# The opening of a transformer layer: modulation and the first token half first, then two tile pairs of products in one run

## The chip, the cores and the metric

The kernel runs on one core of a Trainium2 chip. TensorE multiplies matrices into PSUM; VectorE, ScalarE and GpSimd work elementwise; SyncE and ScalarE issue the transfers from HBM that are named here. The metric is the device time of one execution in microseconds (us). Three timed runs of the kernel before took 1918.53, 1914.31 and 1918.40 us, median 1918.4. The profiled execution is a fourth, of 1915.77 us; its span from the first to the last recorded instruction is 1914.0 us.

## What the kernel computes

One encoder layer on x of 1024 tokens by 1024 channels in float32: a half-step SwiGLU feed-forward, a mixer (convolution and attention), and a second half-step feed-forward. Each is modulated by a conditioning vector c. Cut to what the change touches:

```python
c_act = jax.nn.silu(c)
mod = (c_act @ w_ada[l] + b_ada[l]).reshape(B, N_SUBLAYERS, 3, D)    # 3 x (shift, scale, gate)

def post_norm_sublayer(x, mod, weight, f, g, b):
    shift, scale, gate = mod[:, 0, None, :], mod[:, 1, None, :], mod[:, 2, None, :]
    y = f(x * (1.0 + scale) + shift)
    return layer_norm(ALPHA * x + weight * (1.0 + gate) * y, g, b)

def swiglu(h, w_in, w_out):                     # h: 1024 x 1024, w_in: 1024 x 5632
    gate, up = jnp.split(h @ w_in, 2, axis=-1)
    return (jax.nn.silu(gate) * up) @ w_out
```

Ahead of the first product stand shift and scale of the first sub-layer: 2048 columns of `w_ada`, 8 MB. With them h = x * A + B is made, A = 1 + scale and B = shift, one number per channel.

## The kernel before

**Products.** The first projection h @ w_in runs in 22 tile pairs j (128 gate columns and 128 up columns each). For each pair the 2x2 block product (two halves of the channels, two halves of the tokens) is done with seven products instead of eight, and each of the seven in four channel blocks with three float32 terms (high x high, low x high, high x low): 84 products of 128x512 per pair, called p1 to p7 in the code. Their left factors come from the weights: `ah`/`al` (high and low part of the raw weights), and `sf` (sums of weights) with its parts `sh`/`sl`. The right factors come from the tokens: for each channel block kk, `r_kbh`/`r_kbl` are the parts of the first token half's h, `r_kb` those of one quarter of the second half's h, and `r_kt1h/l` and `r_kt3h/l` those of the differences t12 and t34 between the two halves' h (T1 to T4). A high part is a cast on ScalarE, the low part the rest on VectorE (`split`). Sums of products are gathered in PSUM under names as fi_0A, fi_0S (tile 0), fi_1A (tile 1).

**The opening.** There are four column blocks kk of 256 channels. For each: `first_ada` fetches its `w_ada` columns (four transfers of 512 KB), `first_x` both token halves (`xc`, two of 512 KB); `first_mod` sums eight 128-row pieces of `w_ada` times `c_act`, some columns on VectorE (`ada0a`) and some on TensorE (128x1 products into `ada0p`), and VectorE adds the bias to get two columns of B and two of A. `first_t` transposes both token halves on TensorE, `first_h` applies A and B on ScalarE and VectorE, `right_first`, `right_second` and `right_third` make the right factors, with GpSimd doing most of the subtractions, and `go(k)` issues the 12 products of this block for four of tile 0's seven products (A11, A12, S2, S1). Then `in_phase` does the rest of tile 0, tile 1 and so on; VectorE and ScalarE apply the gate and make the next tile's weight factors beside it.

**What sets the order.** The order of issue is written out by hand in `SEQ` (line 44): `a0` fetches block 0's columns, `M03` computes them (the last digit sets how many of four columns VectorE sums), `w0` fetches tile 0's weights, `x0` the tokens, `G0` and `S0` make weight factors, `H0` is transposes and h, `R0...` the right factors (a letter per step for VectorE or GpSimd), `g0` the products. Each engine then takes its instructions in the order of its own queue, and waits by semaphores for others; a scheduler places instructions within these queues. All transfers named here are in SyncE's queue, in the order of `SEQ`; `slot` and the pools give buffers, and a transfer into a buffer waits until its last reader is through. Tile 1's weights are fetched after the last of `SEQ`, and their factors are issued after block 3's last split.

Of the kernel before, what the change touches and what calls it, by code (L numbers as in the profile page):

```python
# [14 lines left out]
P = 128  # L16
# [27 lines left out]
SEQ = "a0 M03 w0 x0 G0 a1 H0d x1 R0VGVGV M12 x2 a2 H1 M24 S0 g0 a3 R1VGVGG H2 g1 x3 R2VGVGG M33 H3d R3VVVGV g2 g3"  # L44
# [4 lines left out]
def layer_kernel(ctx, tc, a, out):  # L49
# [39 lines left out]
    S.activation(c_act, c_raw, AF.Silu)  # L89
# [216 lines left out]
    def in_load(wp, s, w_in, j):  # L306
# [6 lines left out]
        for dst, src in ((ra[:, 0], k1[:, :, g]), (ra[:, 1], k2[:, :, g]), (rb, k1[:, :, u]), (ra[:, 2], k2[:, :, u])):  # L313
            SY.dma_start(dst, src)
# [9 lines left out]
    def in_sums(wp, s, j, raws, left, eng=V, order=(0, 1)):  # L324
# [3 lines left out]
        sf = [wp.tile([P, 2, 4, P], F32, tag="sf", bufs=2, name=f"sf{s}_{j}_{i}") for i in range(2)]  # L328
        eng.tensor_tensor(sf[0][:, 0], rb, ra[:, 2], ALU.add)
        eng.tensor_tensor(sf[0][:, 1], sf[0][:, 0], ra[:, 0], ALU.subtract)  # L330
        eng.tensor_tensor(sf[1][:, 0], ra[:, 0], rb, ALU.subtract)
        eng.tensor_tensor(sf[1][:, 1], ra[:, 1], sf[0][:, 1], ALU.subtract)
# [333 lines left out]

    x_in = a["x"][0]
    with pool("p1a") as wp:
# [4 lines left out]

        def first_ada(kk):
            raws = []
            for m in range(2):
                for q in range(2):
                    name = f"ada0_{kk}_{m}{q}"
                    if kk == 0 or kk == 3 and m == 1:
                        raw = slot(name, (P, 4, 256), F32)  # L680
                    else:
                        raw = wp.tile([P, 4, 256], F32, tag="sl" if q else "sh", bufs=3, name=name)
                    SY.dma_start(raw, w_ada[:, 4 * q : 4 * q + 4, m * D + kk * 256 : m * D + (kk + 1) * 256])
                    raws.append(raw)
            return raws

        def first_x(kk):
            cols = slice(kk * 256, (kk + 1) * 256)
            xc = []
            for half in range(2):  # L690
                x = slot(f"xc{kk}_{half}", (P, 4, 256), F32)
                SY.dma_start(x, x_in[half * H : (half + 1) * H, cols].rearrange("(t p) n -> p t n", p=P))
                xc.append(x)
            return xc

        def first_mod(kk, raws, n):

            ps = wide(f"ada0p{kk}")
            if n:
                acc = wp.tile([P, 2, 256], F32, tag="ada_acc", bufs=1, name=f"ada0a{kk}")  # L700
            parts = [(m, max(0, 4 - n - 2 * m) * P) for m in (0, 1)]
            for j in range(KD):
                for m, lo in parts:
                    if lo >= 256:
                        continue
                    raw, dst = raws[2 * m + j // 4][:, j % 4, lo:], acc[:, m, lo:]
                    if j == 0:
                        V.tensor_scalar(dst, raw, c_act[:, 0:1], None, ALU.mult)
                    else:
                        V.scalar_tensor_tensor(dst, raw, c_act[:, j : j + 1], dst, ALU.mult, ALU.add)  # L710
            for m, lo in parts:
                for e in range(2):
                    es = slice(e * P, (e + 1) * P)
                    o = ps[:, 2 * m + e : 2 * m + e + 1]
                    if e * P >= lo:
                        PE.matmul(o, lhsT=acc[:, m, es], rhs=ones[:, 0:1], start=True, stop=True)
                        continue
                    for j in range(KD):
                        PE.matmul(
                            o, lhsT=raws[2 * m + j // 4][:, j % 4, es], rhs=c_act[:, j : j + 1],  # L720
                            start=j == 0, stop=j == KD - 1,
                        )
            ks = slice(2 * kk, 2 * kk + 2)
# [3 lines left out]
        def first_t(kk, xc, half):  # L727
            ps = wide(f"hT0_{kk}_{half}")
            for e in range(2):
                for i in range(4):  # L730
                    o = e * H + i * P
                    PE.transpose(ps[:, o : o + P], xc[half][:, i, e * P : (e + 1) * P], ident)
            return ps

        def first_h(kk, ps, half, HD):
            h = slot(f"h0_{kk}_{half}", dt=F32)
            k = 2 * kk
            h_of(h[:, 0], ps[:, 0:H], A0, B0, k)
            if HD:
                V.tensor_scalar(h[:, 1], ps[:, H:T], A0[:, k + 1 : k + 2], B0[:, k + 1 : k + 2], ALU.mult, ALU.add)  # L740
            else:
                h_of(h[:, 1], ps[:, H:T], A0, B0, k + 1)
            return h

        def early(wp, s, w_in, ops):
            order = (("A11", "B11"), ("A12", "B21"), ("S2", "T2"), ("S1", "T1"))
            begun = {}
            ada, xs_, hs, w, L0 = {}, {}, {}, [], {}

            def go(k):  # L750
                for left, right in order:
                    if left not in begun:
                        begun[left] = bank(f"fi{s}_0{left}")
                    product(begun[left], L0[left], ops[right], (k,))

            for tok in SEQ.split():
                c, k, v = tok[0], int(tok[1]), tok[2:]
                if c == "a":  # L760
                    ada[k] = first_ada(k)
                elif c == "x":
                    xs_[k] = first_x(k)
                elif c == "w":
                    w.append(in_load(wp, s, w_in, 0))
                elif c == "G":
                    L0.update(in_gate(wp, s, 0, w[0]))
                elif c == "S":
                    in_sums(wp, s, 0, w[0], L0, G if v else V)
                elif c == "M":  # L770
                    first_mod(k, ada[k], int(v))
                elif c == "H":
                    for half in range(2):
                        hs[k, half] = first_h(k, first_t(k, xs_[k], half), half, v == "d")
                elif c == "R":
                    e = [{"V": V, "G": G}[n] for n in v]
# [690 lines left out]
```

## Time and profile before

| | us |
|---|---|
| Timed runs, median (1914.31 to 1918.53) | 1918.4 |
| Profiled execution | 1915.77 |
| Its span | 1914.0 |
| TensorE busy | 1828.2 (96%) |
| VectorE busy | 1463.4 (76%) |
| ScalarE busy | 773.6 (40%) |
| GpSimd busy | 325.6 (17%) |
| First product of tile 4 starts at | 141.7 |

The mean granted clock of TensorE is 0.979 of full speed. In the profile's rows PE is TensorE, PEld its weight loads (they lie beside PE), DVE is VectorE, ACT ScalarE, POOL GpSimd, SP SyncE; L140 is line 140 of the kernel. A row in order of time begins with the start and the duration in us; in square brackets stands how long the engine had nothing to do before it, and what ended that. A product's duration includes the way through the array, so that products overlap; the distance of their starts (the pitch) is what one costs in a dense run. The same names (r_0bh, fi_0A) return in the second feed-forward, so a count of 4 for a name can hold instructions of both.

### The profile page before, as it was taken

The page shows a single profiled execution, that of the slowest core. Times are in us where ns is not written, and L with a number is a line of the kernel's source. Part 1 is how long each engine was busy: PE and PEld are TensorE (multiplying, and loading weights), DVE is VectorE, ACT ScalarE, POOL GpSimd, SP SyncE. Part 2 cuts the span into 40 slices and gives each one's busy share as a digit, 9 for nine tenths or more (in the row PEclk, how much of TensorE's full clock was granted, in tenths as well). Part 3 has the DMA queues.
Part 4 walks back from the last instruction along what each step waited for, and adds up shares of the span by engine and source line. Part 5 has one row for each costly group of instructions (what it writes and reads, how often), then busy time and mean ns, then how long its engine had stood idle before and what let it go on. Part 6 is the DMA issues. An engine that isn't in the chain of part 4 may idle for free. (4 is left out here: it accounts for less than half of the span.)

```text
span 1914.0 us, 23141 instructions
## 1 busy us (share of the span) xinstructions
PE 1828.2 (96%) x8562; PEld 1513.0 (79%) x8562; DVE 1463.4 (76%) x1982; ACT 773.6 (40%) x1233; POOL 325.6 (17%) x259
## 2 busy tenths in 40 slices
PE   5899999999999999999999889979999999999997
PEld 5688888888888878878788677857888888888886
DVE  8867667766698878999888768688777565569888
ACT  3423333332445442133277664353333333354540
POOL 3200000000000020057667541260000000000001
PEclk7899999999999999999999999989999999999999
DMA  8536555442885324111000014125555333188432
GB/s 254 165 99 208 163 161 175 158 149 83 296 301 165 113 61 163 46 35 33 11 2 1 12 45 154 67 67 170 168 172 177 121 110 127 39 285 281 127 121 72
DMA packets 203696, 246.76 MB, mean 129 GB/s; under 512 B 14122, under 2 KB 124831, under 8 KB 203582
## 3 DMA queue, kind: packets, MB, share of 16 engines
q1 hardware_dynamic: 200234, 235.81, 38.6%
q0 software_dynamic: 2112, 7.34, 1.0%
q10 hardware_dynamic: 1236, 2.13, 0.3%
q8 instruction: 67, 1.10, 0.2%
q14 instruction: 47, 0.39, 0.1%
HBM read 188.08 MB, written 57.15 MB: 128 GB/s over the span
## 5 line engine op out<-in xcount | busy, mean ns | idle before, releaser
L563 PE MATMUL fo<-wr,gl 128*128 128x512 f32 x1848 | 422.5, 390 | 0.5 <-DVE pv L606 0.4
L563 PEld LDWEIGHTS fo<-wr,gl 128*128 128x128 f32 x1848 | 346.2, 188 | 74.8 <-DVE pv L606 0.8
L140 DVE TENSOR_TENSOR sl<-sf,sh 128x1024 fp32r<-128x1024 f32 x87 | 109.3, 1257 | 118.5 <-ACT sh L139 118.5
L139 ACT CAST sh<-sf 128x1024 fp32r<-128x1024 f32 x88 | 92.7, 1054 | 210.0 <-issue 35.8
L910 DVE SCALAR_TENSOR_TENSOR cacc<-u,convw,cacc 128x1009 f32<-128x1009 f32 (+14 forms) x120 | 151.5, 1324 | 0.2
L373 POOL DMA_DIRECT2D gd<-gf x8 | 4.6, 573 | 824.4 <-DVE gf L439 823.9
L140 DVE TENSOR_TENSOR gl<-gr,gl 128x512 fp32r<-128x512 f32 x148 | 102.3, 698 | 7.2 <-ACT gl L139 5.8
L139 ACT CAST gl<-gr 128x512 fp32r<-128x512 f32 x148 | 90.5, 618 | 23.2 <-DMA gr<-gd 16.5
L153 DVE SCALAR_TENSOR_TENSOR ada<-adaw,c_act,ada 128x512 f32<-128x512 f32 x98 | 73.3, 748 | 32.9 <-DMA adaw<-in_w_ada_dram 31.9
L215 POOL TENSOR_TENSOR rr<-rv,mhalf 128x1 f32<-128x1 f32 x24 | 21.8, 909 | 410.3 <-DVE rv L213 408.9
L1036 DVE TENSOR_REDUCE mx<-sc 128x1 f32<-128x1024 f32 x64 | 76.3, 1216 | 19.2 <-PE sc L1034 19.2
L1038 ACT ACTIVATE p<-sc,mx 128x1024 f32<-128x1024 f32 x64 | 71.6, 1122 | 45.1 <-DVE mx L1036 44.9
L139 ACT CAST ah<-ra 128x1536 fp32r<-128x1536 f32 x44 | 65.1, 1479 | 58.0 <-DMA ra<-in_ffn_w_in_dram 14.3
L140 DVE TENSOR_TENSOR al<-ra,ah 128x1536 fp32r<-128x1536 f32 x44 | 77.1, 1752 | 1.6 <-ACT ah L139 1.4
L401 ACT ACTIVATE gf<-gf 128x512 f32<-128x512 f32 x44 | 27.8, 632 | 120.8 <-DVE gf L400 114.9
L139 ACT CAST wr<-wa 128x512 fp32r<-128x512 f32 x66 | 41.2, 624 | 74.3 <-PE fo L563 73.7
L140 DVE TENSOR_TENSOR wr<-wa,wr 128x512 fp32r<-128x512 f32 x66 | 45.5, 690 | 26.6 <-ACT wr L139 26.3
L891 PE MATMUL glu<-hm,gluh 128*128 128x512 f32 x256 | 65.6, 391 | 0.0
L1090 POOL TENSOR_TENSOR p<-p,p 128x1024 f32<-128x1024 f32 x27 | 65.0, 2408 | 1.8
L139 ACT CAST wr<-wb 128x512 fp32r<-128x512 f32 x66 | 40.2, 620 | 60.4 <-PE fo L563 49.7
L1107 PE MATMUL av<-vf,aT 128*128 128x128 f32 x512 | 63.2, 277 | 1.0 <-ACT cacc L1172 1.0
L1107 PEld LDWEIGHTS av<-vf,aT 128*128 128x128 f32 x512 | 60.6, 194 | 1.5 <-ACT cacc L1172 1.3
(3490 smaller groups left out, 4735.9 us busy)
## 6 DMA issues: line engine op xcount, KB each, us to landing
gr<-gd SPq DMA_DIRECT2D x148, 256.0 KB, 3.4
ra<-in_ffn_w_in_dram SPq DMA_DIRECT2D x132, 256.0 KB, 3.7
adaw<-in_w_ada_dram SPq DMA_DIRECT2D x56, 512.0 KB, 3.9
gd<-gf SPq DMA_DIRECT2D x102, 256.0 KB, 2.1
rb<-in_ffn_w_in_dram SPq DMA_DIRECT2D x44, 256.0 KB, 3.7
wb<-in_ffn_w_out_dram SPq DMA_DIRECT2D x44, 256.0 KB, 5.0
wa<-in_ffn_w_out_dram SPq DMA_DIRECT2D x44, 256.0 KB, 5.1
gd<-s SPq DMA_DIRECT2D x40, 256.0 KB, 2.0
```

Of the source, the lines that this page charges most:

```text
L139: a = S.copy(hi, x)
L140: b = eng.tensor_tensor(lo, x, hi.bitcast(F32), ALU.subtract)
L153: V.scalar_tensor_tensor(acc, raw[:, jj], c_act[:, n : n + 1], acc, ALU.mult, ALU.add)
L215: G.tensor_tensor(r, v, mhalf[:, 0:1], ALU.pow)
L401: S.activation(c0, c0, AF.Silu)
L563: PE.matmul(ps, lhsT=g[:, x, ts_], rhs=w[:, y], start=n in (1, 2, 3) and k == i == 0, stop=k == NK - 1 and i == 2, skip_group_check=n not ...
L891: PE.matmul(q[2 * m + h], lhsT=w[:, m * P : (m + 1) * P], rhs=hm[k][h][:, x], start=k == 0 and n == 0, stop=k == KD - 1 and n == 2,)
L910: V.scalar_tensor_tensor(acc[:, lo_t:hi_t], u[:, lo_t + sh : hi_t + sh], convw[:, i, jj : jj + 1], acc[:, lo_t:hi_t], ALU.mult, ALU.add,)
L1036: V.tensor_reduce(mx_, ps, axis=AX.X, op=ALU.max, negate=True)
L1038: S.activation(pe, ps, AF.Exp, bias=mx_, accum_out=sm[:, e : e + 1])
L1090: last = G.tensor_tensor(p0, p0, p1, ALU.add)
L1107: PE.matmul(ps[:, 0:P], lhsT=aT[:, kt], rhs=vf[kt][:, h * P : (h + 1) * P], start=kt == 0, stop=kt == 7)
```

## The change

The fetches are put in another order: first, for each block, eight transfers of 256 KB of `w_ada` and the first token half; then the second halves of blocks 0 and 1, tile 1's weights, and the second halves of blocks 2 and 3. Tile 0's weights are fetched by ScalarE's queue, after `c_act`. `first_mod` treats all four columns alike: VectorE sums 2n of the eight pieces over 512 columns (n = 3 in all blocks: six pieces), TensorE adds the other two and the sum, and ScalarE adds the bias of each column out of PSUM. Only the first token half is transposed there. Nothing of `go(k)` is left; a block's TensorE work is issued after the columns of the block before. What follows is in `mid`, which `in_phase` calls with the steps of the first two tiles: their products in one run, with the second halves' transposes between them and all subtractions on VectorE. `rows`, a pool of one row buffer, is allocated earlier, and t12 of block 0 lies in it. `in_sums` can make its two pairs of sums at different times.

```diff
-SEQ = "a0 M03 w0 x0 G0 a1 H0d x1 R0VGVGV M12 x2 a2 H1 M24 S0 g0 a3 R1VGVGG H2 g1 x3 R2VGVGG M33 H3d R3VVVGV g2 g3"
+NV = (3, 3, 3, 3)
...
+            for q in range(4):
+                raw = slot(f"ada0_{kk}_{q}", (P, 2, 2, 256), F32)
+                for m in range(2):
+                    src = w_ada[:, 2 * q : 2 * q + 2, m * D + kk * 256 : m * D + (kk + 1) * 256]
+                    SY.dma_start(raw[:, :, m], src)
...
         def first_mod(kk, raws, n):
 
-            ps = wide(f"ada0p{kk}")
...
-            V.tensor_tensor(B0[:, ks], ps[:, 0:2], bcol(0, 0)[:, ks], ALU.add)
-            V.scalar_tensor_tensor(A0[:, ks], ps[:, 2:4], 1.0, bcol(0, 1)[:, ks], ALU.add, ALU.add)
+            ps = bank(f"ada0p{kk}")
+            acc = slot(f"ada0a{kk}", (P, 2, 2, 256), F32)[:, 0]
+            for j in range(2 * n):
+                raw = raws[j // 2][:, j % 2]
+                if j == 0:
+                    V.tensor_scalar(acc, raw, c_act[:, 0:1], None, ALU.mult)
+                else:
+                    last = V.scalar_tensor_tensor(acc, raw, c_act[:, j : j + 1], acc, ALU.mult, ALU.add)
+            for i in range(4):
+                m, es = i // 2, slice(i % 2 * P, (i % 2 + 1) * P)
+                o = ps[:, i : i + 1]
+                for j in range(2 * n, KD):
+                    PE.matmul(
+                        o, lhsT=raws[j // 2][:, j % 2, m, es], rhs=c_act[:, j : j + 1], start=j == 2 * n, stop=False
+                    )
+                pe = PE.matmul(o, lhsT=acc[:, m, es], rhs=ones[:, 0:1], start=n == 4, stop=True)
+                k = 2 * kk + i % 2
+                to, bias = ((B0, bcol(0, 0)), (A0, bada1))[m]
+                S.activation(to[:, k : k + 1], o, AF.Identity, bias=bias[:, k : k + 1], scale=1.0)
+            return last.ins, pe.ins
...
+            with tc.issue_after(c_silu.ins):
+                raws = [in_load(wp, s, w_in, 0, S)]
+            ada, xb = [], []
+            for kk in range(4):
+                ada.append(first_ada(kk))
+                xb.append(first_x(kk, 0))
+            xc = [first_x(kk, 1) for kk in range(2)]
+            raws.append(in_load(wp, s, w_in, 1))
+            xc.extend(first_x(kk, 1) for kk in range(2, 4))
+            hb, L = [], [{}, {}]
+            for kk in range(4):
+                with tc.issue_after(columns) if kk else nullcontext():
+                    summed, columns = first_mod(kk, ada[kk], NV[kk])
+                    hb.append(first_h(kk, xb[kk], 0))
+                copied, rest = right_first(f"r0_{kk}", ops, hb[kk])
...
+            with tc.issue_after(first["pe"]):
+                st[0][1]()
+                hc.extend(first_h(kk, first["xc"][kk], 1) for kk in range(2))
+                with tc.issue_after(flipped[-1]):
+                    st[0][2]()
+                for kk in range(4):
...
+                    V.tensor_tensor(t[:, 0], h[:, 0], b[:, 0], ALU.subtract)
+                    V.tensor_tensor(t[:, 1], h[:, 1], t[:, 0], ALU.subtract)
+                    t12.append(t)
+                    if kk:
+                        copied, rest = right_t(f"r0_{kk - 1}", ops, 1, t12[kk - 1])
...
+            for kk in range(5):
+                if kk < 4:
+                    b, h, t = hb[kk], hc[kk], t12[kk]
+                    right_b22(f"r0_{kk}", ops, h)
+                    V.tensor_tensor(h[:, 0], h[:, 1], h[:, 0], ALU.subtract)
+                    V.tensor_tensor(h[:, 1], b[:, 1], t[:, 1], ALU.subtract)
+                if kk:
+                    copied, rest = right_t(f"r0_{kk - 1}", ops, 3, hc[kk - 1])
+            for n in (7, 3, 4):
+                st[0][n]()
...
+            for n in (7, 3, 4):
+                st[1][n]()
```

VectorE's queue before, from block 0's right factors on. `ada0a_296` and `ada0a_362` are the sums of blocks 1 and 2, `r_0t1l` and `r_0t3l` low parts of differences:

```order
L140 TENSOR_TENSOR r_0bl<-h_0_0_255,r_0bh 128x1024
L710 SCALAR_TENSOR_TENSOR ada0a_296<-ada_1_11_244,c_act,ada0a_296 128x256 x2
L140 TENSOR_TENSOR r_0t1l<-r_0t_278,r_0t1h 128x1024
L140 TENSOR_TENSOR r_0b_288<-h_0_1_267,r_0b_288 128x512
L724 TENSOR_TENSOR B_107<-ada0p_295,bada 128x2
L725 SCALAR_TENSOR_TENSOR A_106<-ada0p_295,bada 128x2
L708 TENSOR_SCALAR ada0a_362<-ada_2_00_329,c_act 128x256
L140 TENSOR_TENSOR r_0t3l<-r_0t_285,r_0t3h 128x1024
L710 SCALAR_TENSOR_TENSOR ada0a_362<-ada_2_00_329,c_act,ada0a_362 128x256 x3
```

VectorE's queue after, from the end of block 1's sums (`ada0a_325`) over block 2's (`ada0a_365`) to block 2's low part:

```order
L712 SCALAR_TENSOR_TENSOR ada0a_325<-ada_1_1_213,c_act,ada0a_325 128x512 x2
L712 SCALAR_TENSOR_TENSOR ada0a_325<-ada_1_2_216,c_act,ada0a_325 128x512 x2
L142 TENSOR_TENSOR r_1bl<-h_1_0_357,r_1bh 128x1024
L710 TENSOR_SCALAR ada0a_365<-ada_2_0_224,c_act 128x512
L712 SCALAR_TENSOR_TENSOR ada0a_365<-ada_2_0_224,c_act,ada0a_365 128x512
L712 SCALAR_TENSOR_TENSOR ada0a_365<-ada_2_1_227,c_act,ada0a_365 128x512 x2
L712 SCALAR_TENSOR_TENSOR ada0a_365<-ada_2_2_230,c_act,ada0a_365 128x512 x2
L142 TENSOR_TENSOR r_2bl<-h_2_0_397,r_2bh 128x1024
```

Before, pieces of one block's sums stood between low parts of another's factors. Now all sums of block 1 come first, then r_1bl, and behind it all sums of block 2; the adds that make A and B are gone from this queue.

TensorE's queue before, the first products of tile 0 (fi_0A, fi_0S) between transposes (hT) and the columns of blocks 1 and 2 (`ada0p`):

```order
L352 MATMUL fi_0A_399<-r_0bh,ah_0_234 128x512
L732 MATMUL hT_1_0_337<-ident,xc_0_270 128x128 x7
L716 MATMUL ada0p_295<-ones,ada0a_296 128x1 x2
L732 MATMUL hT_1_0_337<-ident,xc_0_270 128x128
L352 MATMUL fi_0A_399<-r_0bl,ah_0_234 128x512
L352 MATMUL fi_0A_399<-r_0bh,al_0_235 128x512
L352 MATMUL fi_0A_403<-r_0bh,ah_0_234 128x512
L352 MATMUL fi_0A_403<-r_0bl,ah_0_234 128x512
L352 MATMUL fi_0A_403<-r_0bh,al_0_235 128x512
L732 MATMUL hT_1_1_349<-ident,xc_1_272 128x128 x8
L352 MATMUL fi_0S_407<-r_0t1h,sh_0_0_391 128x512
L352 MATMUL fi_0S_407<-r_0t1l,sh_0_0_391 128x512
```

TensorE's queue after, from the last columns of block 3 (`ada0p_404`) on:

```order
L717 MATMUL ada0p_404<-c_act,ada_3_3_247 128x1 x2
L720 MATMUL ada0p_404<-ones,ada0a_405 128x1
L717 MATMUL ada0p_404<-c_act,ada_3_3_247 128x1 x2
L720 MATMUL ada0p_404<-ones,ada0a_405 128x1
L360 MATMUL fi_0A_444<-r_0bh,ah_0_306 128x512
...
L360 MATMUL fi_0A_444<-r_3bh,ah_0_306 128x512
L731 MATMUL hT_0_1_460<-ident,xc_1_252 128x128 x5
L360 MATMUL fi_0A_444<-r_3bl,ah_0_306 128x512
L360 MATMUL fi_0A_444<-r_3bh,al_0_307 128x512
L731 MATMUL hT_0_1_460<-ident,xc_1_252 128x128 x3
L731 MATMUL hT_1_1_472<-ident,xc_1_254 128x128 x8
L360 MATMUL fi_0A_484<-r_0bh,ah_0_306 128x512
```

All columns stand ahead of the first product, and the second halves' transposes (hT_0_1, hT_1_1) stand behind it.

TensorE's queue before, at the first products with the last difference, r_3t3 (`sh_0_1` and `sl_0_1` are weight factors of tile 0):

```order
L352 MATMUL fi_0S_407<-r_2t3h,sl_0_1_396 128x512
L352 MATMUL fi_0S_407<-r_3t3h,sh_0_1_395 128x512
L352 MATMUL fi_0S_407<-r_3t3l,sh_0_1_395 128x512
L352 MATMUL fi_0S_407<-r_3t3h,sl_0_1_396 128x512
L352 MATMUL fi_0S_411<-r_0b_288,sh_0_1_395 128x512 x2
```

TensorE's queue after, at the same products:

```order
L360 MATMUL fi_0S_600<-r_3b_675,sh_0_1_320 128x512 x2
L360 MATMUL fi_0S_600<-r_3b_675,sl_0_1_321 128x512
L360 MATMUL fi_0A_444<-r_3t3h,sh_0_1_320 128x512
L360 MATMUL fi_0A_444<-r_3t3l,sh_0_1_320 128x512
L360 MATMUL fi_0A_444<-r_3t3h,sl_0_1_321 128x512
L360 MATMUL fi_0A_444<-r_0t3h,ah_0_306 128x512
```

The first product that reads r_3t3l is the 119th of the run after the change, with both tiles' first four products of the seven and tile 0's p7 around it. Before, it stood among tile 0's alone.

## Rows read from the trace of the kernel before

**Rows 1.** Stages: length, busy us (instructions) by engine, clock, DMA share, GB/s

```profile
5.00:20.00 15.00, 9.96 (x53) 9.47 (x53) 12.43 (x27) 3.96 (x4) 1.00 (x1) 1.00 1.12 337
20.00:30.00 10.00, 7.39 (x36) 6.41 (x36) 8.97 (x13) 3.56 (x4) 4.24 (x4) 0.55 1.10 348
30.00:51.70 21.70, 14.21 (x49) 11.29 (x48) 21.52 (x34) 9.43 (x12) 8.97 (x5) 0.58 0.59 184
...
65.20:75.30 10.10, 7.96 (x16) 4.50 (x17) 8.69 (x11) 5.58 (x7) 2.25 (x2) 0.51 0.17 48
75.30:102.10 26.80, 26.80 (x118) 21.89 (x117) 25.43 (x35) 9.89 (x13) 0.00 (x0) 0.99 0.57 162
...
141.70:1914.00 1772.30, 1713.05 (x8062) 1419.55 (x8061) 1353.32 (x1821) 721.02 (x1169) 296.41 (x236) 0.99 0.39 125
```

**Rows 2.** TensorE in time: start us, us, instruction [idle before <-releaser]

```profile
30.25 0.63 PE L352 MATMUL fi_0A<-r_0bh,ah 128*128 128x512 f32 x1
30.68 0.63 PE L352 MATMUL fi_0A<-r_0bl,ah 128*128 128x512 f32 x1
...
58.92 1.04 PE L732 MATMUL hT<-ident,xc 128*128 128x128 f32 x8
59.71 0.47 PE L352 MATMUL fi_0A<-r_2bh,al 128*128 128x512 f32 x1
...
65.18 1.10 PE L352 MATMUL fi_0A<-r_3bh,ah 128*128 128x512 f32 x2 [3.40 <-ACT r_3bh L139]
...
70.16 1.22 PE L352 MATMUL fi_0S<-r_3t1h,sh 128*128 128x512 f32 x2 [0.77 <-ACT r_3t1h L139]
```

**Rows 3.** VectorE in order of time, its kinds of instruction

```profile
10.01 2.56 DVE L710 SCALAR_TENSOR_TENSOR ada0a<-ada,c_act,ada0a 128x256 f32<-128x256 f32 x5
13.68 0.16 DVE L724 TENSOR_TENSOR B<-ada0p,bada 128x2 f32<-128x2 f32 x1 [1.10 <-PE ada0p L716]
...
55.78 2.28 DVE L140 TENSOR_TENSOR r_2bl<-h,r_2bh 128x1024 fp32r<-128x1024 f32 x1
...
79.40 1.22 DVE L140 TENSOR_TENSOR sl<-sf,sh 128x1024 fp32r<-128x1024 f32 x1
80.53 0.68 DVE L417 TENSOR_TENSOR p<-fi_0S,p 128x512 f32<-128x512 f32 x1
81.13 1.22 DVE L140 TENSOR_TENSOR sl<-sf,sh 128x1024 fp32r<-128x1024 f32 x1
...
91.83 0.48 DVE L151 TENSOR_SCALAR ada<-adaw,c_act 128x512 f32<-128x512 f32 x1
...
96.21 0.75 DVE L153 SCALAR_TENSOR_TENSOR ada<-adaw,c_act,ada 128x512 f32<-128x512 f32 x1
...
98.68 1.53 DVE L153 SCALAR_TENSOR_TENSOR ada<-adaw,c_act,ada 128x512 f32<-128x512 f32 x2
```

**Rows 4.** First products of tiles 2, 3, 4: count, ns, first and last start

```profile
L352 PE MATMUL fi_2A<-r_0bh,ah x4: 389/389/389, 102.1 to 1311.3; 128*128 128x512 f32 x4
...
L352 PE MATMUL fi_3A<-r_0bh,ah x4: 388/389/389, 121.2 to 1330.5; 128*128 128x512 f32 x4
...
L352 PE MATMUL fi_4A<-r_0bh,ah x4: 389/389/476, 141.7 to 1349.5; 128*128 128x512 f32 x4
```

**Rows 5.** TensorE in order of time, first modulation columns and transposes

```profile
12.63 1.01 PE L716 MATMUL ada0p<-ones,ada0a 128*128 128x1 f32 x4 [3.33 <-DVE ada0a L710]
14.83 1.54 PE L732 MATMUL hT<-ident,xc 128*128 128x128 f32 x6 [1.19 <-DMA xc<-in_x_dram]
```

**Rows 6.** ScalarE in order of time, its kinds of instruction

```profile
2.69 0.21 ACT L89 ACTIVATE c_act<-c_raw 128x8 f32<-128x8 f32 x1
13.29 1.47 ACT L139 CAST ah<-ra 128x1536 fp32r<-128x1536 f32 x1 [10.39 <-DMA ra<-in_ffn_w_in_dram]
...
18.82 1.03 ACT L139 CAST r_0bh<-h 128x1024 fp32r<-128x1024 f32 x1
...
30.18 1.45 ACT L251 ACTIVATE h<-hT,B,A 128x512 f32<-128x512 f32 x2 [3.84 <-DVE A L725]
```

More of the change, by code (lines that the diff above doesn't have):

```diff
@@ L2 @@
+from contextlib import nullcontext
 import concourse.bass as bass
@@ L327, in in_sums @@
             eng = G
[L328 to L332, printed above, removed]
+        if order[0] == 0:
+            left["sf"] = [wp.tile([P, 2, 4, P], F32, tag="sf", bufs=2, name=f"sf{s}_{j}_{i}") for i in range(2)]
+        sf = left["sf"]
+        if 0 in order:
+            eng.tensor_tensor(sf[0][:, 0], rb, ra[:, 2], ALU.add)
+            eng.tensor_tensor(sf[0][:, 1], sf[0][:, 0], ra[:, 0], ALU.subtract)
+        if 1 in order:
+            eng.tensor_tensor(sf[1][:, 0], ra[:, 0], rb, ALU.subtract)
+            eng.tensor_tensor(sf[1][:, 1], ra[:, 1], sf[0][:, 1], ALU.subtract)
         for i in order:
@@ L664, in out_phase @@
             after(1, k)
+    rows = tc.alloc_tile_pool(name="rows", bufs=1, reuse_waits="tile", side="right")
     x_in = a["x"][0]
@@ L672, in layer_kernel @@
         B0 = const.tile([P, KD], F32, name="B0")
+        bada1 = const.tile([P, KD], F32, name="bada1")
+        V.tensor_scalar(bada1, bcol(0, 1), 1.0, None, ALU.add)
         def first_ada(kk):
             raws = []
[L676 to L684, printed above, removed]
@@ L727, in first_t, with first_x @@
-        def first_t(kk, xc, half):
+            for q in range(4):
[3 more added lines that the diff above has]
+                    SY.dma_start(raw[:, :, m], src)
+                raws.append(raw)
+            return raws
+        def first_x(kk, half):
+            x = slot(f"xc{kk}_{half}", (P, 4, 256), F32)
+            src = x_in[half * H : (half + 1) * H, kk * 256 : (kk + 1) * 256]
+            SY.dma_start(x, src.rearrange("(t p) n -> p t n", p=P))
+            return x
@@ L728, in first_t, with first_h @@
+        def first_h(kk, x, half):
             ps = wide(f"hT0_{kk}_{half}")
@@ L731, in first_t @@
                     o = e * H + i * P
-                    PE.transpose(ps[:, o : o + P], xc[half][:, i, e * P : (e + 1) * P], ident)
-            return ps
-        def first_h(kk, ps, half, HD):
+                    flipped[:] = [PE.transpose(ps[:, o : o + P], x[:, i, e * P : (e + 1) * P], ident).ins]
             h = slot(f"h0_{kk}_{half}", dt=F32)
[L737 to L742, printed above, removed]
+            for e in range(2):
+                h_of(h[:, e], ps[:, e * H : (e + 1) * H], A0, B0, 2 * kk + e)
@@ L743, in first_h @@
             return h
+        first, flipped = {}, []
         def early(wp, s, w_in, ops):
[L746 to L776, printed above, removed]
-                    right_first(f"r0_{k}", ops, hs[k, 0], e[0])
-                    t12 = right_second(f"r0_{k}", ops, hs[k, 0], hs[k, 1], e[1], e[2])
-                    last = right_third(f"r0_{k}", ops, hs[k, 0], hs[k, 1], t12, e[3], e[4])
-                elif c == "g":
-                    go(k)
```

85 lines of the change are left out of this document (41 added, 44 removed).

## The prediction

> **What bounds the kernel now.** I read the stage table first [rows 1]. From 75.3 us on TensorE is busy 26.80 of 26.80 us, and from 141.7 us 1713.05 of 1772.30, at a granted clock of 0.99: what counts there is the number of products and their pitch. The change touches only what comes before. Between 20 and 51.7 us the granted clock is about half (0.55, 0.58), and a product takes 0.43 us from its start to the next one's, 30.25 to 30.68 [rows 2]. VectorE is busy 21.52 of 21.70 us in the stretch from 30, and the DMA engines only 0.59 of it: VectorE sets the pace, not the fetch. Part of its load is its neighbour's: at 55.78, in a time when GpSimd subtracts, a 128x1024 low part takes 2.28 us, and at 79.40, with GpSimd at rest, 1.22 [rows 3]. Then TensorE stands still for 3.40 us ahead of 65.18 [rows 2], and the next 10.1 us run at a clock of 0.51 [rows 1].
>
> Tile pairs start at 102.1, 121.2 and 141.7 us for tiles 2, 3 and 4 [rows 4]. One pair is 84 products, and 121.2 - 102.1 = 19.05 us (0.227 per product). Tile 3 takes 20.5, so 1.5 us more, for convolution constants and modulation columns between its products. The instruction order is the same in both kernels from tile 3's first product on, and ahead of tile 4 both have 336 products and 64 transposes. So the question is one number: when does tile 4's first product start, 141.7 us now.
>
> **The change part by part.** After it, products start only when all four column blocks of modulation are through. I call that moment T0.
>
> Block 0. The first token half has the same 3.7 MB ahead of it, so it lands as now, at 14.8 [rows 5]. Eight transposes at half clock: 6 took 1.54, the pitch is 0.215, so 1.65 us, to 16.5. Then four modulation columns. TensorE makes one, ScalarE adds the bias from PSUM (a 128x1 instruction), and since all four share a bank, TensorE's next column waits for ScalarE's read. Two raw products and one of ones: now four columns take 1.1 us from VectorE's last add to VectorE's read, 12.57 to 13.68 [rows 3, 5], so 0.35 for the first and 0.2 for each further single product. I take 0.45 for the first, since its raw products are done, 0.85 for each later one (three products and the hand-over), and 0.25 for ScalarE's part: 0.7, then 1.1 each. The third column is read at 16.5 + 2.9 = 19.4. Then h, the fourth column's read 0.17, and h again (two take 1.45), the high part 1.05 and a hand-over 0.1 [rows 6]: 22.2. VectorE then makes three 128x1024 low parts at a pitch of 1.13 (79.40 to 80.53 [rows 3]), of which two are the weights': 25.6.
>
> Blocks 1 to 3. VectorE adds six eighths of the fetched weights: one 128x512 at 0.48 and five dependent ones at 1.53 - 0.75 = 0.78 [rows 3], 4.4 us in all, to 30.0 for block 1. What is queued behind it decides the period: the low part r_1bl stands in VectorE's queue ahead of block 2's adds, and it waits for columns (2.9), h and the fourth column (1.62), and the high part (1.15), which is 5.7 us without work for VectorE. The period is 5.7 + 1.1 + 4.4 = 11.2. Block 3's adds end at 30.0 + 2 x 11.2 = 52.4. The last column comes 3.7 later: **T0 = 56.1**. The fetch is not in the way: weights, 4 x 2.5 MB of blocks and what else precedes come to 11.5 MB, 33 us at 348 GB/s [rows 1], and block 3's adds start at 48. ScalarE now issues tile 0's four weight fetches itself; it has 10.39 us without work there [rows 6], so they cost nothing.
>
> Cost of the unknown. A 128x1 ScalarE instruction from PSUM isn't in the trace. From below it is bounded by VectorE's 128x2, 0.16, and from above by ScalarE's 128x512 from PSUM, 0.73 (half of 1.45); the nearest row is ScalarE's own 128x8, 0.21 [rows 3, 6], which I take. Some 16 of them are on the path to T0: 16 x (0.16 - 0.21) = -0.8 and 16 x 0.52 = +8.3 us are the ends. [...]
>
> From T0 to tile 4. Four pairs of 84 products: 4 x 19.05 = 76.2. Tile 3's extras 1.5. The second halves' 32 transposes, now in the dense part: 8 took 0.79 at full clock (58.92 to 59.71 [rows 2]), 3.2. The clock: I take half for the columns' stage, as between 20 and 51.7, and a dense start at 70.16 got full clock at 75.3 [rows 1, 2], 5.1 us later: 12 products at 0.43 instead of 0.23, 2.4 in all. Stalls: GpSimd's 16 instructions are now VectorE's, without the slow-down by the neighbour. VectorE can begin them when the first transposed second half is through ScalarE, some ten products and five transposes at half clock and one h after T0: 4.3 + 1.0 + 0.8 and hand-overs, T0 + 7. Up to the low part of the last difference, r_3t3l, it has 24 instructions of 128x512 at 0.60 (80.53 to 81.13; 14.4), nine of 128x1024 at 1.14 (10.3), one half as long again (1.7), and two of the gate row at 0.4 (0.8; the kind at 91.83) [rows 3]: 27.2, and 0.4 for results that the next instruction waits for, T0 + 34.6. TensorE comes to the product that needs it, its 119th, at 118 x 0.227 + 2.4 + 3.2 = T0 + 32.4. Wait 2.2. For the other first uses (tile 1's A22 and its second pair of sums, tile 2's first weights) I add 1.5, as VectorE and ScalarE run without a gap there: 3.7. Between no stall and twice that is the range of this term.
>
> Sum: 76.2 + 1.5 + 3.2 + 2.4 + 3.7 = 87.0; 56.1 + 87.0 = 143.1 against 141.7, **1.4 us later**. Where the gain goes: the 3.40 us of standing still and the half clock of 20 to 75 are gone, but the 48 products of tile 0 that lay in that time are now paid after it. Behind T0 the fetch has one new place: the gate row's fetch waits in SyncE's queue for a slot that VectorE frees at about T0 + 28, and tile 3's weights stand behind it. They have tile 2's 19 us of products as cover; without it 1 to 2 us.
>
> The profiled execution took 1915.8 us (span 1914.0); the median of the runs is 1918.4. I put the change on their middle, 1917.1: **1918.5 us**. About 0.3%, 5.75 us, is what a measurement can tell from no change.
>
> **The rivals.** (A) *The fetch sets the pace.* If the blocks overlap, VectorE works on one block's adds while the others' columns run, a block costs 1.1 + 4.4 = 5.5, adds end at 41, and T0 is 44 to 45: 12 us less, 1906.5. Against it is the queue order above (r_1bl ahead of block 2's adds); for it only that the data is there. (B) *The clock stays full.* The rows show full clock between 5 and 20 us with TensorE busy 9.96 of 15, and 0.55 from 20 on [rows 1]. If columns and transposes hold it, 12 column waits shrink by 0.3, and the 2.4 of the cold start go: 6 us less, 1912.5. (C) *Slower.* Place: the wait for r_3t3l. If VectorE is another 2 us late there (a dependent pair of subtractions per block waits on its own result), TensorE stands for 4.2 us. The one idle time with a fall behind it is the 3.40 us ahead of 65.18; if such a one comes, 10.1 us at half pitch follow [rows 1, 2], 24 products, 24 x 0.2 = 4.8. Then 2.0 + 4.8 = 6.8 more, 1925.3. [...] Against (C): my sum has only 2.2 there, and no row shows that so short a gap decides. (D) *It doesn't do what it says:* column reads near 0.5 rather than 0.21 keep TensorE and ScalarE alternating, 16 x 0.3 = 5 us later, 1923.5, and VectorE idle still longer.
>
> **How the numbers follow.** Forecast 0.55; A 0.07; B 0.14; C 0.15; D 0.09. Faster than 1912.6: A, half of B, a little of the forecast: 0.15. Slower than 1924.2: C, a third of D, a little of the forecast: 0.20. Within: 0.65. The forecast's own range is 1914.5 to 1922.5 (stalls 0 to 7.4). The whole range leaves out A and the far end of the column price: 1911 to 1928.
>
> **What would show it.** TensorE's first product at about 56 us and tile 4's at about 143. Blocks 11 us apart, with VectorE waiting some 5.7 us for ScalarE's high part before each r_1bl, r_2bl, r_3bl, and TensorE's columns waiting on ScalarE. Granted clock near 0.5 until about 61, then 1.0. A wait of some 2 us ahead of the first product with r_3t3l. I am wrong if blocks come 5 to 6 us apart (A), if the load stage shows full clock (B), if a stretch at half clock follows after 88 (C), or if tile 4 onward differs by more than 2 us from now.

## The result and the profile after

The changed kernel took 1930.22 us (median of four runs, 1929.06 to 1930.87) beside 1917.88 for the kernel before: 1.0067 times as long, 95% interval 1.005 to 1.0085. It is slower by 12 us; the forecast was 1918.5 with a range of 1911 to 1928. The profiled execution has a span of 1929.1 us, 15.1 more than before.

Nearly all of it lies ahead of tile 4. The first row is the first product of tile 0, the second that of tile 4, in the changed kernel (count; shortest, median and longest in ns; first and last start):

```profile
L360 PE MATMUL fi_0A<-r_0bh,ah x4: 398/476/774, 67.8 to 1265.6; 128*128 128x512 f32 x4
...
L360 PE MATMUL fi_4A<-r_0bh,ah x4: 389/389/476, 155.9 to 1363.3; 128*128 128x512 f32 x4
```

Tile 4 starts at 155.9 us and not at 141.7 [rows 4]: 14.2 later. T0, the first product, is at 67.8; I had put it at 56.1. From there to tile 4 are 88.1 us, and I had put 87.0. So the stretch from T0 to tile 4 came out within 1.1 us of the sum, and the opening took 11.7 us more than I thought. The stages of the changed kernel (columns as in [rows 1]):

```profile
20.00:30.00 10.00, 6.24 (x28) 5.67 (x27) 4.49 (x6) 5.28 (x8) 0.00 (x0) 1.00 1.10 348
30.00:51.70 21.70, 10.39 (x44) 9.57 (x44) 9.53 (x13) 4.17 (x9) 0.00 (x0) 1.00 1.11 314
51.70:67.80 16.10, 9.53 (x43) 8.79 (x42) 5.38 (x7) 4.68 (x9) 0.00 (x0) 1.00 0.00 1
```

Between 30 and 51.7 VectorE was busy 21.52 us [rows 1] and is now busy 9.53. The fetch moves 314 GB/s to 51.7 and then nothing: in the 16 us before T0 every byte that the opening needs is there. No engine is full and nothing is fetched, so it is a chain that sets the time. One link of it is block 1's columns on TensorE, in order of time (start us, us, instruction, and the idle time ahead with what ended it):

```profile
34.38 0.59 PE L720 MATMUL ada0p<-ones,ada0a 128*128 128x1 f32 x2 [7.44 <-DVE ada0a L712]
35.32 1.02 PE L717 MATMUL ada0p<-c_act,ada 128*128 128x1 f32 x4 [0.35 <-ACT B L723]
36.19 0.56 PE L720 MATMUL ada0p<-ones,ada0a 128*128 128x1 f32 x2
37.11 1.01 PE L717 MATMUL ada0p<-c_act,ada 128*128 128x1 f32 x4 [0.35 <-ACT B L723]
```

A round, from one column's first product to the next one's, is 37.11 - 35.32 = 1.79 us, where I had 1.1. L717 is two products and the row says x4; L720 is one and the row says x2. The group of the columns' tile says it for the whole opening:

```profile
L717 PE MATMUL ada0p<-c_act,ada x64: 344/352/374, 12.8 to 67.2; 128*128 128x1 f32 x64
...
L720 PE MATMUL ada0p<-ones,ada0a x32: 213/352/372, 18.5 to 67.6; 128*128 128x1 f32 x32
```

The program has 2 x 4 x 4 = 32 products on L717 and 16 on L720. Each float32 product of one column stands as two instructions. The row on which I priced a column, "L716 ... x4" in 1.01 us [rows 5], was therefore two columns and not four. The kernel before has the same two for one: the last digits of `M03`, `M12`, `M24` and `M33` make 3 + 2 + 4 + 3 = 12 products of ones, and its trace has 24 records of them:

```profile
L716 PE MATMUL ada0p<-ones,ada0a x24: 250/352/373, 8.5 to 55.4; 128*128 128x1 f32 x24
```

What the longer rounds do to a block is seen on ScalarE and VectorE. ScalarE in block 1, in order of time:

```profile
36.80 0.26 ACT L723 ACTIVATE B<-ada0p,bada 128x1 f32<-128x1 f32 x1 [1.53 <-PE ada0p L720]
38.59 0.26 ACT L723 ACTIVATE A<-ada0p,bada 128x1 f32<-128x1 f32 x1 [1.53 <-PE ada0p L720]
38.88 0.78 ACT L253 ACTIVATE h<-hT,B,A 128x512 f32<-128x512 f32 x1
40.38 0.26 ACT L723 ACTIVATE A<-ada0p,bada 128x1 f32<-128x1 f32 x1 [0.72 <-PE ada0p L720]
40.68 0.78 ACT L253 ACTIVATE h<-hT,B,A 128x512 f32<-128x512 f32 x1
41.49 1.04 ACT L141 CAST r_1bh<-h 128x1024 fp32r<-128x1024 f32 x1
```

And VectorE from the end of block 1's sums to block 2's low part:

```profile
30.43 3.90 DVE L712 SCALAR_TENSOR_TENSOR ada0a<-ada,c_act,ada0a 128x512 f32<-128x512 f32 x5
42.56 1.23 DVE L142 TENSOR_TENSOR r_1bl<-h,r_1bh 128x1024 fp32r<-128x1024 f32 x1 [8.24 <-ACT r_1bh L141]
43.70 0.48 DVE L710 TENSOR_SCALAR ada0a<-ada,c_act 128x512 f32<-128x512 f32 x1
44.22 3.90 DVE L712 SCALAR_TENSOR_TENSOR ada0a<-ada,c_act,ada0a 128x512 f32<-128x512 f32 x5
56.36 1.22 DVE L142 TENSOR_TENSOR r_2bl<-h,r_2bh 128x1024 fp32r<-128x1024 f32 x1 [8.24 <-ACT r_2bh L141]
```

VectorE waits 8.24 us for each high part, not 5.7: a period of 13.8 us (42.56 to 56.36), not 11.2. A read of one column is 0.26 us, close to the 0.21 that I took. The second half of h waits for the fourth column (0.72 us of idle time at 40.38), which I had hidden beside the first half.

### The profile page after: what moved, and what is told of

Same layout as the page of the kernel before. It is cut to its first block, busy times and chain, and to the rows that moved or that the text cites. A ratio compares the mean times of both kernels' runs of the same rounds, so it can differ in the third digit from the quotient of the medians.

```text
span 1929.1 us, 23148 instructions
## 1 busy us (share of the span) xinstructions
PE 1828.7 (95%) x8570; PEld 1514.3 (78%) x8570; DVE 1451.3 (75%) x1952; ACT 780.8 (40%) x1254; POOL 298.3 (15%) x243
## 5 line engine op out<-in xcount | busy, mean ns | idle before, releaser
L141 ACT CAST wr<-wa 128x512 fp32r<-128x512 f32 x66 | 41.2, 624 | 73.9 <-PE fo L571 71.8
```

Of the source, the lines that this page charges most:

```text
L141: a = S.copy(hi, x)
```

## The experiments

Each was timed beside the kernel before, whose medians in the four sessions were 1915.5, 1916.1, 1916.7 and 1916.2, and 1917.9 beside the change; so between sessions the ratios are the safer comparison. T0 is the start of the first product of the dense run; where products stand between the blocks there is none.

| Run | T0 | tile 4 | time | ratio to before, 95% interval |
|---|---|---|---|---|
| before | | 141.7 | | |
| the change | 67.8 | 155.9 | 1930.2 | 1.0067 [1.005, 1.0085] |
| e1_four_sums | 62.1 | 151.0 | 1923.3 | 1.0036 [1.0023, 1.0049] |
| e2_banks | 53.1 | 141.9 | 1914.6 | 0.9995 [0.9986, 1.0003] |
| e3_sums_ahead | 54.3 | 141.5 | 1913.8 | 0.9986 [0.9975, 0.9997] |
| e4_warm (one run) | 62.8 | 150.0 | 1922.1 | |
| e5_banks_ahead | 46.8 | 132.3 | 1906.6 | 0.9945 [0.993, 0.9959] |
| e6_all_three | 46.1 | 134.9 | 1910.8 | 0.9968 [0.9956, 0.998] |
| e7_interleave | | 132.3 | 1906.4 | 0.9946 [0.9931, 0.9961] |
| e8_reads_after | 64.4 | 152.5 | 1927.0 | 1.0055 [1.004, 1.007] |
| e9_products_between | | 150.4 | 1923.8 | 1.0039 [1.0025, 1.0053] |
| e10_interleave_raw_first | | 133.4 | 1907.9 | 0.9958 [0.9944, 0.9972] |
| e11_x_first | | 131.4 | 1903.1 | 0.9932 [0.9917, 0.9947] |
| e12_banks_ahead_x_first | 47.5 | 133.5 | 1906.6 | 0.9943 [0.9929, 0.9956] |

In the nine with a T0, tile 4 comes 85.5 to 88.9 us behind it, wherever T0 lies between 46 and 68. So the opening's length passes into the kernel's time to within some 3 us, and the break-even is a T0 of about 53.6 (141.7 - 88.1). From tile 4 to the end the fourteen profiles take 1768.6 to 1774.6 us, 1772.3 before and 1773.2 in the change.

**e1_four_sums: fewer products per column.**

```diff
-NV = (3, 3, 3, 3)
+NV = (4, 4, 4, 4)
```

> VectorE sums all eight pieces (NV = 4), so a column is one product of ones and not three products. My theory (a column's round of 1.79 us, made of three float32 products of two passes each, 0.43 us a product, and the hand-over to ScalarE and back, sets the opening): a round falls to 0.94 us, the chain from VectorE's last sum to its low part from 8.24 to about 5.5 us, against 1.6 us more of sums per block; the first dense product starts at about 62 us instead of 67.8, and the time falls by about 5.7 us to 1924.5. Rival (the opening is slow because no products lie in its waits, and the columns' length does not matter): the first dense product is not earlier, or later by the 3 x 1.6 us of sums, 1930 to 1935 us.

```profile
33.16 0.58 PE L720 MATMUL ada0p<-ones,ada0a 128*128 128x1 f32 x2 [7.23 <-DVE ada0a L712]
34.10 0.59 PE L720 MATMUL ada0p<-ones,ada0a 128*128 128x1 f32 x2 [0.35 <-ACT B L723]
```

In these rows of block 1 on TensorE a round is 0.94 us, as expected, and T0 came to 62.1 with 1.6 us more of sums in every block: the time to 1923.3 where 1924.5 was expected. Two products fewer take 0.85 us off a round of 1.79.

**e2_banks: a bank for each column.**

```diff
-            ps = bank(f"ada0p{kk}")
...
-                o = ps[:, i : i + 1]
+                o = bank(f"ada0p{kk}_{i}")[:, 0:1]
```

> Each of a block's four columns has a PSUM bank of its own, so TensorE makes the raw products of all four before VectorE's sum is there, and does not wait for ScalarE's read between columns. My theory: after the last sum four products of 0.43 us remain, the chain from last sum to low part falls from 8.24 to about 4.6 us in each block, the first dense product starts at about 53 us, tile 4 at about 141, and the time is about 1915.6 us, 2 us under the kernel before. Rival (no products in the waits is what costs): the first dense product stays within 3 us of 67.8, the time above 1927.

```profile
46.48 1.31 PE L730 MATMUL hT<-ident,xc 128*128 128x128 f32 x5
51.25 1.87 PE L719 MATMUL ada0p<-ones,ada0a 128*128 128x1 f32 x8 [3.46 <-DVE ada0a L711]
52.98 0.45 PE L730 MATMUL hT<-ident,xc 128*128 128x128 f32 x1
53.08 0.77 PE L360 MATMUL fi_0A<-r_0bh,ah 128*128 128x512 f32 x1
```

In block 3 on TensorE only the four products of ones (x8) remain behind the sum; the other eight have gone ahead into the waiting time. A block's period falls from 13.80 to 10.23 us (these products of blocks 2 and 3 start at 41.02 and 51.25). With VectorE's own work of a block as in the change (13.80 - 8.24 = 5.56), its wait for each high part is an estimated 4.67 us in place of 8.24. T0 is 53.1, as expected, and the time that of the kernel before.

**e3_sums_ahead: the other link of the chain.**

```diff
+                if kk < 3:
+                    with tc.issue_after(summed):
+                        acc, summed = first_sums(kk + 1, ada[kk + 1], NV[kk + 1])
+                with tc.issue_after(summed):
+                    copied, rest = right_first(f"r0_{kk}", ops, hb[kk])
```

> Block k + 1's sums stand in VectorE's queue ahead of block k's low part (columns as in the changed kernel). My theory: the period of a block is then TensorE's own, four rounds, two raw products and eight transposes, about 8.5 us instead of 13.8; the first dense product starts at 50 to 52 us, and the time is 1912 to 1915 us. Rival (the columns alone set the pace whatever VectorE's order): period 13.8, 1930 us. Rival (the fetch): blocks wait for their columns of w_ada, the first dense product not before 55 us, 1917 or more.

T0 54.3 and not 50 to 52, the time 1913.8 as expected. Blocks 0 to 1 and 2 to 3 follow each other in the 8.3 to 8.4 us that TensorE itself needs. Between 1 and 2 TensorE waits 5.15 us for VectorE, in whose queue tile 0's weight factors (`sl`) stand between the pieces of block 2's sums:

```profile
40.18 0.58 PE L724 MATMUL ada0p<-ones,ada0a 128*128 128x1 f32 x2 [5.15 <-DVE ada0a L711]
...
35.53 2.36 DVE L142 TENSOR_TENSOR sl<-sf,sh 128x1024 fp32r<-128x1024 f32 x2 [2.06 <-ACT sh L141]
37.81 2.32 DVE L711 SCALAR_TENSOR_TENSOR ada0a<-ada,c_act,ada0a 128x512 f32<-128x512 f32 x3
```

**e4_warm: the clock.** Sixteen products that nobody reads, ahead of the transposes of blocks 1 to 3; the kernel computes nothing else than the change.

```diff
+                if i == 0 and kk:
+                    ah = first["ah"]
+                    fill = bank(f"fill{kk}")
+                    for j in range(16):
+                        PE.matmul(fill, lhsT=ah[1][:, j % 4], rhs=ah[0].rearrange("p a b -> p (a b)"), start=j == 0, stop=j == 15)
```

> Sixteen products of 128x512 whose result nobody reads stand ahead of the transposes of blocks 1 to 3, in time in which TensorE waits. Theory that the low clock in the opening is what makes a column round 1.79 us: the rounds after them run at full clock, 0.22 us a product instead of 0.43, a round is about 1.2 us, and the first dense product starts 3 to 5 us earlier. My theory (two passes and the hand-over make the round; a few products do not hold the clock through four short columns): the rounds stay above 1.5 us, and the first dense product is within 3 us of 67.8 or later by the products' own time.

```profile
34.97 0.61 PE L717 MATMUL ada0p<-c_act,ada 128*128 128x1 f32 x4 [0.35 <-ACT B L728]
35.43 0.36 PE L725 MATMUL ada0p<-ones,ada0a 128*128 128x1 f32 x2
36.15 0.66 PE L717 MATMUL ada0p<-c_act,ada 128*128 128x1 f32 x4 [0.35 <-ACT B L728]
36.66 0.57 PE L725 MATMUL ada0p<-ones,ada0a 128*128 128x1 f32 x2
37.58 1.01 PE L717 MATMUL ada0p<-c_act,ada 128*128 128x1 f32 x4 [0.35 <-ACT A L728]
```

My expectation failed. Behind the filler the rounds are 1.18 us (34.97 to 36.15) in place of 1.79, and T0 is 5 us earlier. The filler lies in TensorE's wait for VectorE's sum, of which 2.33 and 0.62 us are left in blocks 1 and 2, so that there it costs nothing; in block 3 no wait is left. In block 1 the gain ends at 36.66, where a product takes 0.43 again; in block 3 it lasts through all four columns, whose products of ones start 1.18 to 1.20 us apart (59.01 to 62.57). So a round is three products of two instructions each, at half clock, and the hand-over; the two causes multiply.

**e8_reads_after: the hand-over alone.**

```diff
                 pe = PE.matmul(o, lhsT=acc[:, m, es], rhs=ones[:, 0:1], start=n == 4, stop=True)
+            for i in range(4):
+                m, o = i // 2, ps[:, i : i + 1]
```

> The changed kernel, but ScalarE reads a block's four columns after the last of them, so that TensorE does not wait for ScalarE between two columns; the products are as many as in the change and stand in the same order. Theory that the hand-over to ScalarE and back is what makes a round long: 0.5 us of each of the 15 rounds on the path goes, the first dense product starts 6 to 8 us earlier, about 1922 us. My theory (the three products of two passes each are what makes it long, and a read of one bank waits for the last write to it, so ScalarE begins later by what TensorE saves): the chain from last sum to low part stays at 8 us, the first dense product comes 1 to 2 us earlier, 1927 to 1929 us.

```profile
38.06 0.41 ACT L725 ACTIVATE B<-ada0p,bada 128x1 f32<-128x1 f32 x2 [9.92 <-PE ada0p L720]
38.37 0.41 ACT L725 ACTIVATE A<-ada0p,bada 128x1 f32<-128x1 f32 x2
38.66 1.46 ACT L253 ACTIVATE h<-hT,B,A 128x512 f32<-128x512 f32 x2
```

TensorE's columns take 1.28 us each without the hand-over, three products at 0.43, but ScalarE starts only behind the last. I put that down to the one bank that holds all four; no run separates it from the order of issue, in which all reads now stand behind all products. VectorE's wait falls from 8.24 to 7.69 us; T0 is 3.4 us earlier (0.7 of it because the first token half landed earlier), between the 1 to 2 that I expected and the 6 to 8 of the other theory; 1926.95 us, at the edge of what I expected and 5 from the other theory.

**e9_products_between: are the lost products the cause?**

```diff
+                    begun = {n: bank(f"fi{s}_0{n}") for n in ("A11", "A12")}
+                for n, r in (("A11", "B11"), ("A12", "B21")):
+                    product(begun[n], L[0][n], ops[r], (kk,))
...
-            return L, ({}, {}), mid
+            return L, (begun, {}), mid
```

> The changed kernel with nothing else altered than this: the 6 products per block of A11 and A12 stand between the blocks, in TensorE's waits of 5 us. Theory that the lost products are what made the change slower: all of the 13 us comes back, 1917 us or less. My theory (the length of a block is what made it slower): 18 products at 0.23 us, 4 us, and up to 5 us where the products keep the clock up for the next columns as the filler products did: 1919 to 1925 us.

1923.8 us: some 40% of the loss comes back, tile 4 by 5.5 of 14.2 us. Eighteen products done in the waits are worth an estimated 4.1 of it (18 x 0.227), and 0.8 is an earlier landing of the first token half (15.9 and 16.7). The periods of the blocks hardly move (13.8 and 13.0 us), since behind the six products one round of block 2 is 1.18 us (48.11 to 49.29) and the others of blocks 1 to 3 are still 1.79. So the theory that all 13 us come back fell. But the run gives back only 18 of the 48 products that lay between the blocks before, and what all 48 would be worth it can't say. Shorter blocks alone make up for the loss: e2 and e3 give back none of these products and are level with the kernel before.

**e5, e6: both links.** e5_banks_ahead has the edits of e2 and e3 together; e6_all_three adds NV = (3, 4, 4, 4) and issues tile 0's weight factors a block later.

> Both edits of the two runs before in one: a PSUM bank for each column, and block k + 1's sums ahead of block k's low part. My theory (each took away another part of one chain, so they add until TensorE's own columns, 8 raw products, 8 transposes and 4 products of ones, 7 us a block, set the pace): the first dense product starts at 46 to 48 us, tile 4 at about 135, the time is 1908 to 1910 us. Rival (one resource, the fetch, lies under both, so that they do not add): the first dense product stays at 52 to 54 us, 1914.

> As the run beside it, and VectorE sums all eight pieces in blocks 1 to 3 (NV = 3, 4, 4, 4), tile 0's weight factors issued after block 2's sums. My theory: TensorE has 3.5 us a block left and VectorE 7.1; the first dense product starts at 42 to 43 us, the time is 1903 to 1906 us. Rival (with the products this early the second halves and tile 1's weights are not there, or VectorE's differences are late): the first dense product at 42 to 43, but waits of 3 us or more behind it, 1907 to 1910.

The two edits add: T0 46.8 in e5, and its 1906.6 us is under the 1908 to 1910 I gave. e6's 1910.8 is above both of its ranges. Of its T0 the number, 42 to 43 in both theories, held neither way: T0 46.1, because VectorE's sums are now what ends last. Block 3 on TensorE shows the two things that it waits for, the transposes for their transfer and the products of ones for VectorE:

```profile
38.39 1.94 PE L734 MATMUL hT<-ident,xc 128*128 128x128 f32 x8 [4.09 <-DMA xc<-in_x_dram]
...
44.32 1.84 PE L723 MATMUL ada0p<-ones,ada0a 128*128 128x1 f32 x8 [3.98 <-DVE ada0a L711]
```

Behind T0 e6 needs 88.8 us and e5 85.5. e6's waits there are five of 0.2 to 0.8 us, of which e5 lacks two, 1.0 us together. And e5's products reach the pitch of the full clock sooner. The first two rows are e5's, 2.3 us behind its T0, the last two e6's, where the same comes 5.7 us behind T0:

```profile
49.07 0.40 PE L360 MATMUL fi_0A<-r_1bh,al 128*128 128x512 f32 x1
49.31 0.40 PE L360 MATMUL fi_0A<-r_2bh,ah 128*128 128x512 f32 x1
...
51.24 0.72 PE L360 MATMUL fi_0A<-r_3bl,ah 128*128 128x512 f32 x1
51.80 0.39 PE L360 MATMUL fi_0A<-r_3bh,al 128*128 128x512 f32 x1
```

I estimate 1.6 us for that: e5 has five products at about 0.43 instead of 0.23, e6 eleven and four transposes. The last 0.7 us stay open.

**e7, e10, e11, e12: products between the blocks, and the token half first.** e7 has sums ahead, NV = (3, 4, 4, 4), e8's reads and e9's products; e10 the same with NV = 3 and the raw products of all columns first; e11 is e10 with the edit below; e12 is e5 with it.

```diff
+                if kk:
+                    xb.append(first_x(kk, 0))
                 ada.append(first_ada(kk))
-                xb.append(first_x(kk, 0))
+                if not kk:
+                    xb.append(first_x(kk, 0))
```

> Sums ahead, NV = 3, 4, 4, 4, ScalarE reads a block's four columns after the last of them, and the 6 products per block of tile 0's first two of seven (A11, A12) stand between the blocks again. My theory: the opening is over at the same 42 to 44 us, and 18 products (4.1 us) are already done by then and hold the clock up for some of the columns: 1899 to 1903 us. Rival (products between blocks delay the next block's columns by as much as they save): 1904 to 1907 us.

> Sums ahead, six pieces on VectorE in all blocks, the raw products of all four columns ahead of the four products of ones in one bank, ScalarE's reads after them, and the 6 products per block of A11 and A12 between the blocks. Mine: TensorE has 9.5 us of work a block at half clock and 5 at full, the fetch takes 7.5 a block; the columns are through at 47 to 50 us, and 18 products (4.1 us) are already done: 1904 to 1907 us. Rival (the products keep the clock up from block 1 on): 1900 to 1903 us.

> As the run beside it, and in blocks 1 to 3 the token half is fetched ahead of the block's columns of w_ada, so that its transposes do not wait for the block's last transfer. Mine: transposes lie earlier in TensorE's waits, 1 to 2 us less than the run beside it, 1903 to 1906 us. Rival (the columns' sums, not the transposes, end last, and they now start 1.5 us later): the same or 1 us more.

> A bank for each column and sums ahead, as in e5_banks_ahead, no products between the blocks, and in blocks 1 to 3 the token half fetched ahead of the block's columns of w_ada. Theory that fetching the token half first is worth what the runs e10 and e11 differ by, wherever TensorE waits for it: 4 to 5 us under e5_banks_ahead, about 1902 us. Rival (without products between the blocks the sums end last, and they start 1.5 us later): within 2 us of e5_banks_ahead, 1905 to 1908 us.

e7 and e10 came out 3.4 and 0.9 us above the ranges I gave, e7 within its rival's. That the blocks end later with products between them, by as much as the 18 products gain, would fit, but no run has these edits without the products. e11 is 4.8 us under e10, more than the 1 to 2 expected, but e12 is level with e5 (1906.6 both), as its rival had it. So the token half's place is worth nothing that can be measured where the sums end last, and something with products between. Tile 4 shows only 2.0 us of e11's 4.8 (133.4 and 131.4); the other 2.8 lie behind tile 4 (1772.2 us in e10's profile, 1769.4 in e11's), within the spread that this stretch has in all profiles. All of e5, e7, e11 and e12 are faster than both kernels, by 0.5 to 0.7% of the kernel before; e11 is the lowest, 0.9932. I would build on e5 all the same: e10 and e11 begin a block's four sums in one bank before any of them is ended, and e5 has a bank for each. That is my choice; no run here shows that the shared bank does harm.

## Why the prediction was wrong

- **The step that failed** is the sum for four columns in block 0, "so 0.35 for the first and 0.2 for each further single product". It rests on reading a count of four instructions as four products. At half clock a single product is 0.43 us, a later column 1.79 and not 1.1. The whole of that 0.69 is the price of three products (3 x 0.43 - 3 x 0.2); the hand-over with ScalarE's read is 0.50 us (1.79 - 3 x 0.43), which is what the sum gave it (0.25 and 0.25). It enters three times: block 0's columns (2.4 us), two periods of 13.8 for 11.2 (5.2), and the last column, 5.9 behind the last sum and not 3.7 (2.2). Together 9.8 of T0's 11.7 us.
- **The other 1.9 us** is the token half's landing: "it lands as now, at 14.8". It landed at 16.7, at a like number of bytes ahead of it. The first two rows are its issue in SyncE's queue before and after the change, the third its first use after:

```profile
8.10 2.46 SPq L692 DMA_DIRECT2D xc<-in_x_dram  x2
...
10.37 0.37 SPq L700 DMA_DIRECT2D xc<-in_x_dram  x1
...
16.71 1.97 PE L731 MATMUL hT<-ident,xc 128*128 128x128 f32 x8 [2.88 <-DMA xc<-in_x_dram]
```

  So it is issued 2.3 us later, and lands 6.3 us behind its issue (6.7 before). Where TensorE waits for it in the other runs, it landed at 15.9 (e9) to 17.3 (e12); so the T0 of two single profiles can differ by more than 1 us for this alone. The fetch ahead of it is slower than before: between 4 and 7.5 us it moves 252 GB/s, and 363 in the kernel before. What holds it up was not tried.
- **The bounds were put around the wrong term.** I named the 128x1 read on ScalarE as the unknown cost and gave it -0.8 to +8.3 us. It measured 0.26 and not the 0.21 I took, some 0.8 us in all. The products beside it, for which I had a row, carried the error, and had no bounds at all. The range to 1928 missed by 2 us for that. (By stalls of 0 to 7.4 the forecast's own range is 1914.8 to 1922.2, not 1914.5 to 1922.5; nothing hangs on it.)
- **Right:** the chain and what is queued behind it (the low part ahead of the next sums), the half clock in the columns' stage, and the run after T0 (87.0 forecast, 88.1 measured). That agreement is in part luck. The waits there are 2.7 us and not 3.7, and the cold start 1.9 (nine products from 67.8 to 71.8) and not 2.4, so the other terms came out 2.6 us longer. The wait for r_3t3l was 0.76 us and not 2.2 because TensorE came to it 1.9 us later than worked out, at T0 + 34.3; VectorE was through at T0 + 35.0, where I had 34.6. The longest waits (us in total, times, longest), with that product's row first:

```profile
102.81 0.50 PE L360 MATMUL fi_0A<-r_3t3l,sh 128*128 128x512 f32 x1 [0.76 <-DVE r_3t3l L142]
...
PE fi_0A L360 <- DVE p L425: 0.8, 1, 0.8
PE fi_0A L360 <- DVE r_3t3l L142: 0.8, 1, 0.8
PE fi_0S L360 <- ACT p L420: 0.7, 1, 0.7
```

- **The rivals.** (A) fell: the blocks did not overlap, and the fetch had long been over. (B) fell: the products before T0 had the pitch of the half clock, 0.43 us. (C) fell: no such wait came and no stretch at half clock after 72. (D) had the right place (TensorE and ScalarE alternating), but 5 us as its price, for a reason that the reads' 0.26 us excludes.
- **Where the gain went.** The change did take TensorE's interruptions out of the products. What it put in their place was a chain through three engines that left TensorE idle for 6.6 of the last 16.1 us before T0 and the two others for two thirds of them. e3 and e2 show that the chain is not needed: one order in VectorE's queue, or four PSUM banks, took some 14 us off T0 each.

## What to carry to other kernels

Before a row's count is made a price, compare it with the number of products that the program has on that line; here a float32 product of one column is two records (64 for 32 products on L717), and a float32 transpose one (x8 for a block's eight at 16.71). When work is cleared out of a stage, look for the chain that remains and ask of each engine what stands in its queue ahead of the next round's first step: one low part in front of the sums cost some 13 us of T0 here (67.8 and 54.3 in e3). Columns that several engines hand to each other want banks of their own: that took 14.7 us off T0 (e2), and putting all writes of one bank before the first read only 3.4 (e8).

## What the runs showed that was not expected

The granted clock in the profile's stages reads 1.00 from 20 to 67.8 us of the changed kernel, while its products there have the pitch that the kernel before shows at a granted clock of 0.55 to 0.58, 0.43 us [rows 1, 2]. They have it still in these rows, where the first products of the dense run stand 0.43 us apart and the last two 0.23:

```profile
70.93 0.63 PE L360 MATMUL fi_0A<-r_2bl,ah 128*128 128x512 f32 x1
71.35 0.58 PE L360 MATMUL fi_0A<-r_2bh,al 128*128 128x512 f32 x1
71.78 0.39 PE L360 MATMUL fi_0A<-r_3bh,ah 128*128 128x512 f32 x1
72.01 0.71 PE L731 MATMUL hT<-ident,xc 128*128 128x128 f32 x5
```

So in an opening the column for the clock can stand at full while the engine works at half, and rival (B), which took the 1.00 between 5 and 20 us [rows 1] for a full clock, had nothing behind it: the transposes of [rows 5] had the slow pitch already (0.215 us, and 0.1 at full clock). The pitch of a known instruction is the surer sign. The half clock ended 4.0 us behind the first dense product (67.8 to 71.8); I had taken 5.1 from the kernel before. It is 2.3 us in e5's profile and 5.7 in e6's, so this term alone can move the time by more than 1 us.
